# Conv input product of a diffusion layer on one Trainium2 core: tokens stationary, 512 weight columns streamed, `mod_w` loads in twos

## The chip, the cores and the metric

The kernel runs on one core of a Trainium2 chip. The time is device microseconds (us) from the first to the last instruction of the core, with the launch around it, and the figure that counts is the median of the timed runs. Engines by their names in the profile: PE (TensorE, matmuls; PEld are its weight loads), DVE (VectorE), ACT (ScalarE), POOL (GpSimd), SP (SyncE, which issues the large loads).

## What is computed

One layer over 256 latent tokens of width 2048, in float32: a modulation vector from `c`, a gated short convolution, a layer norm, and a mixture of 16 experts with top 2 of one group.

```
mod = split(silu(c) @ mod_w + mod_b, 6)                      # six vectors of 2048
h = x * (1 + mod[1]) + mod[0]
gate_b, gate_c, val = split(h @ w_in, 3)                     # w_in: 2048 x 6144
o = (gate_b * depthwise_conv3(gate_c * val, w_conv)) @ w_out # w_out: 2048 x 2048
x = layer_norm(ALPHA * x + mod[2] * o)
x = layer_norm(ALPHA * x + mod[5] * moe(x * (1 + mod[4]) + mod[3]))
```

The change is in the product `h @ w_in` (the "input product") and in what stands around it: the gating, the convolution over tokens, and the loads of `mod_w`.

## The kernel before

**Loads.** All weights come through a ring of six SBUF slots (`get`, `RING`), each 3072 float32 per partition, 1.57 MB. SP issues the loads in the order of a list `steps`; a slot is loaded again only when its last reader is done, and a load that waits for its slot holds up all later ones on SP.

**Steps.** The first part of the kernel, up to about 520 us, is that list. Each step has a load and a piece of work: `cin_step` (input product), `cout_step` (output product, `co`), `gemv_cols` and `gemv_rows` (a block of 512 columns of `mod_w` times the vector `silu(c)`, `gv`; its 16 row blocks come in three loads of 6, 6 and 4). `merge` deals the steps of one list between those of another. The input product can only run for those rows of `h` whose modulation is known, so there are five stages over the inner dimension (`KGS` = 2, 2, 4, 4, 4 blocks of 128): while stage i is multiplied for a first half of the channels, the `mod_w` blocks for stage i+1 are loaded and multiplied (`h_mods`), and partial sums are added up in SBUF (`acc_step`, tiles `acc`). The second half of the channels (`full_steps`) then runs with all of `h` at hand and sums in PSUM. The rest of the blocks of `mod_w` (`late`; `EXTRA` of them inside the stages) and the output product `co` are dealt between the steps.

**Precision.** A float32 matmul of the products is three matmuls: weights and tokens are each split into a rounded high part (ACT, `hic`, `hio`) and a low part (DVE, `loc`, `loo`), and high x high, high x low, low x high are summed. `split` does 1024 columns at a time, with two buffers for each part: the split of a piece can begin only when PE is done with the piece before the last. I call such a piece a half.

**Input product.** In `cin_step` 128 x 128 of the weights is the stationary operand and 256 tokens (`hhi`, `hlo`) are streamed, so results come out with channels on the partitions, as the convolution over tokens needs them; `conv_group` works on them directly (`u`, `v`, then `yh` and `yl` for the output product). The output product does it the other way: tokens (`yh`, `yl`) stationary, 512 weight columns streamed.

**Blocks on DVE.** Five of the late blocks of `mod_w` are not multiplied on PE but on DVE (`ON_V`): 15 multiply-adds each (`rows`). They wait in `queue`, and `split` takes two of them after each half.

**Order.** What stands behind what on one engine is not as written: a scheduler reorders the instructions of an engine when the program is built. The order stays fixed at run time, each engine goes through its own in turn.

Of the kernel before, what the change touches and what calls it, by code (L numbers as in the profile page):

```python
# [27 lines left out]
BIG = 1.0e30  # L28

RING = 6  # L30
ACC_GROUPS = 4
YB = 4
DRIP = (1, 6, 3)
EXTRA = [0, 1, 0, 0, 12]
KGS = [2, 2, 4, 4, 4]
BEFORE = 4
EARLY = 3
VN = 2
AT = 1
# [27 lines left out]
def trunk_kernel(  # L67
# [30 lines left out]
    def mm_tile(name):  # L98
        return psum.tile([P, 512], F32, tag="mm", bufs=6, name=name)
# [302 lines left out]
    def mm3(ps, whi, wlo, ahi, alo, start, stop):  # L402
        TE.matmul(ps, whi, ahi, start=start, stop=False)  # L403
        TE.matmul(ps, whi, alo, start=False, stop=False)  # L404
        TE.matmul(ps, wlo, ahi, start=False, stop=stop)  # L405

    def cin_step(k0, nk, g, pss, first, last, then=None, hook=None):
        n = nk * 256

        def load(w):  # L410
            wv = w[:, : 3 * n].rearrange("p (a t c) -> p a t c", a=3, c=256)
            for a in range(3):
                nc.sync.dma_start(wv[:, a], cin[:, a, k0 : k0 + nk, g * 256 : (g + 1) * 256])

        def work(w):
            if first:
                pss.extend(mm_tile(f"ci{k0}_{g}{a}") for a in range(3))
            for a in range(3):
                hi, lo = split(w[:, a * n : (a + 1) * n], n, f"c{k0}_{g}{a}")
                if a == 1 and hook:  # L420
# [7 lines left out]
            if then:  # L428
                then(pss)

        return load, work

    def conv_group(g, gb, gc, val):

        u = p1.tile([P, 2, T], F32, tag="e", bufs=3, name=f"u{g}")
        V.tensor_mul(u.rearrange("p b t -> p (b t)"), val, gc)
        v = p1.tile([P, 2, T], F32, tag="e", bufs=3, name=f"v{g}")
        for b in range(2):
            ct = g * 2 + b
# [7 lines left out]
        V.tensor_mul(vf, vf, gb)  # L447
        yh = p1.tile([P, 2, T], F32R, tag="yhi", bufs=YB, name=f"yh{g}")
        yl = p1.tile([P, 2, T], F32R, tag="ylo", bufs=YB, name=f"yl{g}")
        S.copy(yh.rearrange("p b t -> p (b t)"), vf)  # L450
        V.tensor_sub(yl.rearrange("p b t -> p (b t)"), vf, yh.rearrange("p b t -> p (b t)").bitcast(F32))
        yhi[g], ylo[g] = yh, yl

    accs = [big_tile(f"acc{g}").rearrange("p (a t) -> p a t", a=3) for g in range(ACC_GROUPS)]
    mod2b = p1.tile([P, D], F32, name="mod2b")
    stats = const.tile([P, 2, 4, 6], F32, name="stats")

    def acc_step(i, g, hook=None):
        def then(pss):
            for a in range(3):  # L460
                if i == 0:
                    V.tensor_copy(accs[g][:, a, :], pss[a][:, :])
                else:
                    V.tensor_add(accs[g][:, a, :], accs[g][:, a, :], pss[a][:, :])  # L464
            if i == len(KGS) - 1:
                conv_group(g, accs[g][:, 0, :], accs[g][:, 1, :], accs[g][:, 2, :])
        return cin_step(sum(KGS[:i]), KGS[i], g, [], True, True, then, hook)

    def full_steps(g):
        def then(pss):  # L470
            gcs = p1.tile([P, 512], F32, tag="e", bufs=3, name=f"gcs{g}")
            S.copy(gcs, pss[1][:, :])
            conv_group(g, pss[0][:, :], gcs, pss[2][:, :])
        pss = []
        return [cin_step(kg * 4, 4, g, pss, kg == 0, kg == 3, then if kg == 3 else None) for kg in range(4)]

# [107 lines left out]

    def h_mods(i):
        c0, n = sum(KGS[:i]) * P, KGS[i] * P
        return list(gemv_cols(0, c0, n)) + list(gemv_cols(1, c0, n))

    def h_hook(i):
        def fn():
# [17 lines left out]

    def merge(a, b):

        out, nb = [], 0
        for i, st in enumerate(a):
            out.append(st)
            while nb < (i + 1) * len(b) // len(a):
                out.append(b[nb])
                nb += 1
        return out

    steps = h_mods(0) + [(None, lambda w: h_hook(0)())]
    late = [st for m in (2, 3, 4) for q in range(4) for st in mods(m, q)]
    last = [st for q in range(4) for st in mods(5, q)]
    NK = len(KGS)
    for i in range(NK):
        nxt = h_mods(i + 1) if i < NK - 1 else []
        nxt += late[sum(EXTRA[:i]) : sum(EXTRA[: i + 1])]
        steps += merge([acc_step(i, g) for g in range(ACC_GROUPS - 1)], nxt)
        steps += [acc_step(i, ACC_GROUPS - 1, h_hook(i + 1) if i < NK - 1 else None)]
    late = late[sum(EXTRA) :]  # L630
    rest = []
    for g in range(ACC_GROUPS, CG):
        fs = last_cin = full_steps(g)
        qt = [cout_step(g - 4, j) for j in range(4)] if 4 <= g < 7 else []
        if g < 6:
            rest += fs[:2] + qt + fs[2:]
        elif g == 6:
            rest += fs
        else:
            rest += fs + qt_last  # L640
        qt_last = qt
    steps += merge(rest[:-BEFORE], late) + [(None, lambda w: router_prep())]
# [673 lines left out]
```

## Time and profile before

| | us |
|---|---|
| median of 3 runs | 1300.05 (1299.6 to 1301.11) |
| profiled execution, its own time | 1300.78 |
| its span, first to last instruction | 1299.1 |
| first part: steps up to the router | up to about 520 |
| experts | about 520 to 1270 |

A busy PE is not PE at its peak: matmuls overlap, so a PE that is busy all the time can still be waiting between matmuls. Start-to-start distances say what one matmul costs in a stream. Names are those of the program with buffer numbers left out: `ci<-hhi,hic` writes the sums of the input product from the tokens' and the weights' high parts. An idle time is given with what ended it.

### The profile page before, as it was taken

What the parts mean: (1) busy time and instruction counts of PE and PEld (TensorE: products, weight loads), DVE (VectorE), ACT (ScalarE), POOL (GpSimd) and SP (SyncE); (2) the same over time, 40 slices, a digit from 0 to 9 for tenths busy, and PEclk for the clock granted to TensorE, in tenths of its full rate; (3) what the DMA queues carried; (4) which work ended last, traced back from release to release, by engine and by line L of the source; (5) the groups of instructions that cost most, each with busy time, mean ns of one, the idle gap of its engine ahead of it and who ended that gap; (6) DMA issues with size and microseconds to landing.
All of it is one profiled execution on the core that took longest, in us unless ns stands there. A gap on an engine that the chain in (4) does not pass through costs nothing. (4 is left out here: it accounts for less than half of the span.)

```text
span 1299.1 us, 19675 instructions
## 1 busy us (share of the span) xinstructions
PE 1148.7 (88%) x7871; PEld 755.3 (58%) x7871; DVE 669.4 (52%) x1257; ACT 364.7 (28%) x634; POOL 36.2 (3%) x66
## 2 busy tenths in 40 slices
PE   4999999999999999887789997999689997789982
PEld 2778886878699965543257543674157443444352
DVE  1664555687879978442255642573146431123226
ACT  1332333433344424240035312451026110100020
POOL 1000000000300030000000000000000000000000
PEclk7999999999999999698899999999899999899996
DMA  9999889899999878899998899999999899999991
GB/s 310 372 388 396 301 286 399 305 315 338 348 316 347 306 270 282 366 412 430 429 409 349 321 422 428 405 360 376 428 430 425 338 429 429 429 428 430 429 396 69
DMA packets 151105, 475.61 MB, mean 366 GB/s; under 512 B 11000, under 2 KB 70104, under 8 KB 126688
## 3 DMA queue, kind: packets, MB, share of 16 engines
q1 hardware_dynamic: 145984, 471.89, 92.4%
q10 hardware_dynamic: 5024, 2.40, 0.6%
q8 instruction: 64, 1.05, 0.3%
q14 instruction: 33, 0.27, 0.1%
HBM read 472.16 MB, written 2.10 MB: 365 GB/s over the span
## 5 line engine op out<-in xcount | busy, mean ns | idle before, releaser
L986 PE MATMUL gue<-w,xgp 128*32 128x384 f32 (+1 forms) x1664 | 219.1, 538 | 63.6 <-DMA w<-in_ex_w_up_dram 55.7
L403 PE MATMUL ci<-hhi,hic 128*128 128x256 f32 x768 | 219.6, 287 | 2.3 <-ACT hic L395 1.4
L405 PE MATMUL ci<-hhi,loc 128*128 128x256 f32 x768 | 217.3, 284 | 3.8 <-DVE loc L396 3.6
L404 PE MATMUL ci<-hlo,hic 128*128 128x256 f32 x768 | 216.9, 283 | 0.6 <-DVE hlo L390 0.4
L986 PEld LDWEIGHTS gue<-w,xgp 128*32 128x32 f32 (+1 forms) x1664 | 81.3, 123 | 198.3 <-issue 90.1
L403 PEld LDWEIGHTS ci<-hhi,hic 128*128 128x128 f32 x768 | 145.4, 190 | 14.6 <-issue 8.4
L395 ACT CAST hic<-w 128x1024 fp32r<-128x1024 f32 (+1 forms) x108 | 102.5, 953 | 178.8 <-PE ci L404 153.3
L405 PEld LDWEIGHTS ci<-hhi,loc 128*128 128x128 f32 x768 | 145.1, 189 | 9.4 <-DVE loc L396 6.6
L404 PEld LDWEIGHTS ci<-hlo,hic 128*128 128x128 f32 x768 | 145.5, 189 | 5.4 <-DVE hlo L390 2.3
L396 DVE TENSOR_TENSOR loc<-w,hic 128x1024 fp32r<-128x1024 f32 (+1 forms) x108 | 118.5, 1106 | 34.2 <-ACT hic L395 32.0
L733 DVE TENSOR_TENSOR parts<-w,parts 128x384 fp32r<-128x384 f32 (+1 forms) x168 | 97.8, 612 | 56.8 <-ACT parts L732 55.5
L732 ACT CAST parts<-w 128x384 fp32r<-128x384 f32 (+1 forms) x168 | 89.7, 559 | 79.2 <-PE gue L983 59.5
L1005 ACT COPY gse<-gue 128x384 f32<-128x384 f32 x16 | 7.7, 481 | 313.9 <-PE gue L986 313.9
L858 PEld LDWEIGHTS gap<-ohp,xt 128*128 128x128 f32 x512 | 66.0, 209 | 22.6 <-issue 16.0
L858 PE MATMUL gap<-ohp,xt 128*128 128x128 f32 (+2 forms) x512 | 70.2, 294 | 5.0 <-DVE xgp L826 5.0
L986 PE MATMUL gue<-w,xfp 128*128 128x384 f32 x192 | 71.5, 495 | 1.7 <-DMA w<-in_ex_w_gate_dram 1.7
L273 PE MATMUL gv<-w,sT 128*32 128x512 f32 (+1 forms) x416 | 57.1, 567 | 7.5 <-DMA w<-in_mod_w_dram 7.5
L464 DVE TENSOR_TENSOR acc<-acc,ci 128x512 f32<-128x512 f32 x48 | 32.9, 686 | 58.8 <-PE ci L405 58.6
L1092 DVE TENSOR_TENSOR Y<-dne,m 32x512 f32<-32x512 f32 (+3 forms) x84 | 40.7, 484 | 37.4 <-PE dne L944 34.1
L278 DVE SCALAR_TENSOR_TENSOR rows<-w,sT,rows 128x512 f32<-128x512 f32 x75 | 57.8, 771 | 1.3
L558 PE MATMUL co<-loo,yh 128*128 128x512 f32 x128 | 51.5, 402 | 3.0 <-DVE loo L396 3.0
L826 DVE TENSOR_SCALAR xgp<-gap,GB 128x32 f32<-128x32 f32 (+1 forms) x104 | 31.5, 314 | 43.6 <-ACT xgp L824 43.1
(311 smaller groups left out, 1452.7 us busy)
## 6 DMA issues: line engine op xcount, KB each, us to landing
w<-in_ex_w_gate_dram SPq DMA_DIRECT2D x64, 1536.0 KB, 14.7
w<-in_ex_w_up_dram SPq DMA_DIRECT2D x64, 1536.0 KB, 16.8
w<-in_ex_w_down_dram SPq DMA_DIRECT2D x60, 1536.0 KB, 14.0
w<-in_mod_w_dram SPq DMA_DIRECT2D x48, 1536.0 KB, 8.9
w<-in_conv_in_w_dram SPq DMA_DIRECT2D x84, 512.0 KB, 6.9
w<-in_mod_w_dram SPq DMA_DIRECT2D x22, 1024.0 KB, 8.2
w<-in_conv_out_w_dram SPq DMA_DIRECT2D x16, 1024.0 KB, 6.6
w<-in_conv_in_w_dram SPq DMA_DIRECT2D x24, 256.0 KB, 6.3
```

The source lines that it names most:

```text
L273: TE.matmul(box["ps"][32 * g : 32 * g + 32, :n], sT[:, kt : kt + 1].to_broadcast([P, 32]), ws, start=kt < 4, stop=kt >= 12)
L278: V.scalar_tensor_tensor(out=box["r"][:, :n], in0=ws, scalar=sT[:, kt : kt + 1], in1=box["r"][:, :n], op0=ALU.mult, op1=ALU.add)
L395: S.copy(hi[:, :n], src)
L396: V.tensor_sub(lo[:, :n], src, hi[:, :n].bitcast(F32))
L403: TE.matmul(ps, whi, ahi, start=start, stop=False)
L404: TE.matmul(ps, whi, alo, start=False, stop=False)
L405: TE.matmul(ps, wlo, ahi, start=False, stop=stop)
L558: TE.matmul(pso[h][:, :], yh[:, k, a:b], wl, start=False, stop=False)
L732: S.copy(hi[:, :n], src)
L733: V.tensor_sub(lo[:, :n], src, hi[:, :n].bitcast(F32))
L858: TE.matmul(ps[:, k * n : (k + 1) * n], xn[:, h, (k0 + k) * P : (k0 + k + 1) * P], oh[:, h, :n], start=h == 0, stop=h == 1)
L986: TE.matmul(dst, big[0][:, KF.index(kt), :] if cc == 128 else xg[:, kt, :cc], src, start=st_, stop=sp_)
```

## The change

**Input product.** `cin_step` now holds 128 tokens (`hhi`, `hlo`) stationary and streams 512 weight columns, for two halves of the tokens and part by part (gate_b, gate_c, val): 1152 matmuls of 512 columns take the place of 2304 of 256. Results have tokens on the partitions. `accs` has two groups of 512 channels where there were four of 256; a group's slots are now full in every stage (two steps for a stage of 4). `full_steps` runs one part at a time over all of the inner dimension, in slots of 6, 6 and 4 blocks.

**Convolution.** `conv_group` first transposes u (already gate_c x val) and gate_b back to channels on partitions: 8 matmuls of 128 x 128 with `ident` (`uT`, `bT`) for 256 channels, 64 in all; ACT and DVE then read them from PSUM. The product gate_c x val is done before, on the `acc` tiles. A group's two pairs are two calls, both put in `pending` and run after the next step.

**Loads of `mod_w`.** `runs` binds the first two loads of a block together; `merge` deals such pairs. `EXTRA` goes from [0, 1, 0, 0, 12] loads to [0, 0, 0, 0, 8] pairs and singles (12 loads), so one load that stood in the second stage comes later.

```diff
-    def cin_step(k0, nk, g, pss, first, last, then=None, hook=None):
...
-                for b in range(2):
-                    for k in range(nk):
-                        o = k * 256 + b * P
-                        mm3(pss[a][:, b * T : (b + 1) * T], hi[:, o : o + P], lo[:, o : o + P],
-                            hhi[:, k0 + k, :], hlo[:, k0 + k, :],
-                            first and k == 0 and b == 0, last and k == nk - 1 and b == 1)
+    def cin_step(entries, g, pairs, k_first, k_last, then, hook=None):
...
+                for k in range(0, nk, 2):
+                    hi, lo = split(w[:, o + k * 512 : o + k * 512 + 1024], 1024, f"c{g}{a}{k0 + k}")
+                    for j in range(2):
+                        kt = k0 + k + j
+                        wh, wl = hi[:, j * 512 : j * 512 + 512], lo[:, j * 512 : j * 512 + 512]
+                        for h in range(2):
+                            ps, s = pairs[a][h], slice(h * P, (h + 1) * P)
+                            TE.matmul(ps[:, :], hhi[:, kt, s], wh, start=kt == k_first, stop=False)
+                            TE.matmul(ps[:, :], hhi[:, kt, s], wl, start=False, stop=False)
+                            TE.matmul(ps[:, :], hlo[:, kt, s], wh, start=False, stop=kt == k_last)
...
-    def conv_group(g, gb, gc, val):
-        u = p1.tile([P, 2, T], F32, tag="e", bufs=3, name=f"u{g}")
-        V.tensor_mul(u.rearrange("p b t -> p (b t)"), val, gc)
+    def conv_group(g, pr=0):
+        u = mm_tile(f"uT{g}{pr}")
+        gb = mm_tile(f"bT{g}{pr}")
+        for a, ps in ((2, u), (0, gb)):
+            for b in range(2):
+                for h in range(2):
+                    c = (pr * 2 + b) * P
+                    TE.transpose(ps[:, b * T + h * P : b * T + h * P + P], accs[g][h][:, a, c : c + P], ident)
...
+        if pr == 0:
+            pending.append(lambda: conv_group(g, 1))
...
-    def acc_step(i, g, hook=None):
+    def acc_steps(i, g, hook=None):
...
+            if i == len(KGS) - 1 and a == 2:
+                for h in range(2):
+                    V.tensor_mul(accs[g][h][:, 2, :], accs[g][h][:, 2, :], accs[g][h][:, 1, :])
+                pending.append(lambda: conv_group(g))
...
     def full_steps(g):
...
+            for h in range(2):
+                o = accs[g][h]
+                if a == 2:
+                    V.tensor_mul(o[:, 2, :], pair[h][:, :], o[:, 1, :])
+                else:
+                    S.copy(o[:, a, :], pair[h][:, :])
+            if a == 0:
+                pending.append(lambda: conv_group(g))
...
+        return [cin_step([(a, k0, nk)], g, pairs, 0, KT - 1, then)
+                for a in (1, 2, 0) for k0, nk in ((0, 6), (6, 6), (12, 4))]
...
+    def runs(sts):
+        return [sts[:-1], sts[-1:]]
...
+    rest = fs[:3] + co[0] + fs[3:6] + co[1] + fs[6:] + last_cin + co[2]
```

Three places of the fixed order follow, of before and of after.

On PE, in the stage of the fourth pair of `mod_w` blocks: the matmuls of the first block (`gv` of columns 1536) stand in pieces in before, with products between; these are the second and third piece (five matmuls of a load of which the first stood sixty rows ahead, and six of the next load).

```order
L405 MATMUL ci_02_1386<-hhi,loc_02_1444 128x256
L273 MATMUL gv_1536_1478<-w_1146,sT 32x512 x5
L273 MATMUL gv_1536_1478<-w_1238,sT 32x512 x6
L403 MATMUL ci_10_1495<-hhi,hic_10_1498 128x256
L404 MATMUL ci_10_1495<-hlo,hic_10_1498 128x256
L405 MATMUL ci_10_1495<-hhi,loc_10_1499 128x256
```

After:

```order
L429 MATMUL ci_1054<-loc_1056,hhi 128x512
L430 MATMUL ci_1054<-hic_1055,hlo 128x512
L271 MATMUL gv_1536_1073<-w_852,sT 32x512 x6
L271 MATMUL gv_1536_1073<-w_860,sT 32x512 x6
L428 MATMUL ci_1053<-hic_1091,hhi 128x512
L429 MATMUL ci_1053<-loc_1092,hhi 128x512
```

The twelve matmuls of two loads now stand in one run; in before they are runs of 1 and 11.

On DVE, late in the second half of the channels, where a block is multiplied on DVE (`rows`) beside the input product (`loc` is the low part of a half), before:

```order
L396 TENSOR_TENSOR loc_70_4141<-w_3914,hic_70_4140 128x1024
L278 SCALAR_TENSOR_TENSOR rows_3918<-w_3824,sT,rows_3918 128x512 x2
L396 TENSOR_TENSOR loc_71_4171<-w_3914,hic_71_4170 128x1024
L278 SCALAR_TENSOR_TENSOR rows_4230<-w_3928,sT,rows_4230 128x512 x2
L396 TENSOR_TENSOR loc_72_4201<-w_3914,hic_72_4200 128x1024
L278 SCALAR_TENSOR_TENSOR rows_4230<-w_3928,sT,rows_4230 128x512 x2
L396 TENSOR_TENSOR loc_70_4243<-w_4035,hic_70_4242 128x1024
L278 SCALAR_TENSOR_TENSOR rows_4230<-w_3928,sT,rows_4230 128x512
```

After:

```order
L394 TENSOR_TENSOR loc_2917<-w_2772,hic_2916 128x1024
L276 SCALAR_TENSOR_TENSOR rows_2935<-w_2776,sT,rows_2935 128x512
L276 SCALAR_TENSOR_TENSOR rows_2935<-w_2778,sT,rows_2935 128x512 x4
L250 TENSOR_REDUCE gs_512_2942<-gc_512_2937 128x4
L276 SCALAR_TENSOR_TENSOR rows_2935<-w_2778,sT,rows_2935 128x512
L252 SCALAR_TENSOR_TENSOR modT<-gs_512_2942,T1t 128x4
L394 TENSOR_TENSOR loc_2950<-w_2834,hic_2949 128x1024
L394 TENSOR_TENSOR loc_2968<-w_2834,hic_2967 128x1024
```

Two `rows` stand between halves in before; here five, six with the one behind `gs`, stand between the last half of one slot (`w_2772`) and the first of the next (`w_2834`).

On DVE, where the input product ends and the third quarter of the output product begins (`loo` is the low part of a half of `co`; `rtB`, `rsums`, `rtw` and `gbm` prepare the router), before:

```order
L396 TENSOR_TENSOR loo_4539<-w_4240,hio_4538 128x1024
L451 TENSOR_TENSOR yl_4438<-v_4429,yh_4437 128x512
L485 TENSOR_TENSOR B_101<-B_101,modT 128x16
L565 TENSOR_TENSOR t_4504<-co_4470,mod2b 128x512
L488 TENSOR_TENSOR rtB<-rtw,B_101 128x512
L565 TENSOR_TENSOR t_4507<-co_4471,mod2b 128x512
L489 TENSOR_REDUCE rsums<-rtB 128x20
L490 TENSOR_TENSOR rtw<-rtw,G_100 128x512
L396 TENSOR_TENSOR loo_4555<-w_4240,hio_4554 128x1024
L491 TENSOR_REDUCE rsums<-rtw 128x20
L396 TENSOR_TENSOR loo_4581<-w_4331,hio_4580 128x1024
```

After, the last rows ahead of the half `loo_3355`:

```order
L457 SCALAR_TENSOR_TENSOR v_3255<-uT_3245,T2t,v_3255 128x255
L520 TENSOR_TENSOR rtw<-rtw,G_100 128x512
L460 TENSOR_TENSOR v_3255<-v_3255,bT_3246 128x512
L521 TENSOR_REDUCE rsums<-rtw 128x20
L595 TENSOR_TENSOR t_3320<-co_3286,mod2b 128x512
L464 TENSOR_TENSOR yl_3264<-v_3255,yh_3263 128x512
L595 TENSOR_TENSOR t_3323<-co_3287,mod2b 128x512
L526 TENSOR_TENSOR rb<-rb,rsum 128x20
L527 COPY rsum<-rsum 128x20
L538 TENSOR_TENSOR gbm_3337<-gbT,gbmask 16x512
L538 TENSOR_TENSOR gbm_3343<-gbT,gbmask 16x512
L394 TENSOR_TENSOR loo_3355<-w_3114,hio_3354 128x1024
```

In before one half (`loo_4555`) has seven rows between it and the half ahead. After, `loo_3355` has 22: these eleven, and eleven more like them between the half ahead of it and the first row shown (the end of one pair's convolution, the start of the next one's, `gs`, `modT`, `G`, `B`, `rtB`, one `rsums`).

## Rows read from the trace of the kernel before

**Rows 1.** The page: busy tenths of PE and DMA in 40 slices of the span

```profile
PE   4999999999999999887789997999689997789982
...
DMA  9999889899999878899998899999999899999991
```

**Rows 2.** By stages: window, us, busy PE PEld DVE ACT POOL, PEclk, DMA, GB/s

```profile
28.70:84.60 55.90, 54.12 (x437) 41.82 (x438) 33.13 (x61) 17.37 (x31) 0.00 (x0) 0.96 1.04 373
84.60:132.00 47.40, 46.17 (x359) 36.84 (x357) 27.29 (x38) 16.40 (x20) 0.00 (x0) 1.00 1.07 398
132.00:178.80 46.80, 46.53 (x370) 38.12 (x369) 26.39 (x37) 15.91 (x18) 0.00 (x0) 1.00 0.88 318
178.80:240.50 61.70, 57.26 (x430) 40.38 (x429) 38.56 (x55) 21.98 (x31) 0.00 (x0) 1.00 0.95 348
240.50:449.00 208.50, 204.98 (x1493) 181.99 (x1493) 169.49 (x211) 82.42 (x92) 13.54 (x8) 1.00 0.90 319
449.00:520.00 71.00, 69.16 (x384) 44.49 (x386) 56.19 (x99) 26.57 (x31) 15.13 (x11) 1.00 0.81 286
```

**Rows 3.** Timeline of PE (start, us, instruction): ten products apart, then twelve

```profile
288.90 0.28 PE L403 MATMUL ci<-hhi,hic 128*128 128x256 f32 x1
...
290.08 0.28 PE L404 MATMUL ci<-hlo,hic 128*128 128x256 f32 x1
...
271.19 0.39 PE L557 MATMUL co<-hio,yh 128*128 128x512 f32 x1
...
273.91 0.39 PE L557 MATMUL co<-hio,yh 128*128 128x512 f32 x1
```

**Rows 4.** The same timeline: four transposes and the matmul behind them

```profile
274.59 0.60 PE L250 MATMUL gc<-ident,rows 128*128 128x128 f32 x4
274.95 0.47 PE L557 MATMUL co<-hio,yh 128*128 128x512 f32 x1
```

**Rows 5.** Lines of the first part, by shape: the transposes of the tokens

```profile
L382 PE MATMUL xT<-ident,xt 128*128 128x128 f32 x32 | 5.4, 297 | 0.0
```

**Rows 6.** Timeline of PE: two runs of `gv`, each with the row behind

```profile
145.22 2.77 PE L273 MATMUL gv<-w,sT 128*32 128x512 f32 x22
147.92 0.39 PE L403 MATMUL ci<-hhi,hic 128*128 128x256 f32 x1
...
159.20 1.91 PE L273 MATMUL gv<-w,sT 128*32 128x512 f32 x12
161.04 0.39 PE L405 MATMUL ci<-hhi,loc 128*128 128x256 f32 x1
```

**Rows 7.** Timeline of DVE: a half, three `rows`, the next half

```profile
439.43 1.22 DVE L396 TENSOR_TENSOR loc<-w,hic 128x1024 fp32r<-128x1024 f32 x1 [0.17 <-ACT hic L395]
440.57 2.32 DVE L278 SCALAR_TENSOR_TENSOR rows<-w,sT,rows 128x512 f32<-128x512 f32 x3
442.81 1.22 DVE L396 TENSOR_TENSOR loc<-w,hic 128x1024 fp32r<-128x1024 f32 x1
```

**Rows 8.** Timeline of DVE at the start of the third quarter of `co`

```profile
453.03 0.68 DVE L451 TENSOR_TENSOR yl<-v,yh 128x512 fp32r<-128x512 f32 x1
...
454.91 0.68 DVE L565 TENSOR_TENSOR t<-co,mod2b 128x512 f32<-128x512 f32 x1
455.52 0.74 DVE L489 TENSOR_REDUCE rsums<-rtB 128x20 f32<-128x320 f32 x1
456.16 1.76 DVE L490 TENSOR_TENSOR rtw<-rtw,G 128x512 f32<-128x512 f32 x1
457.85 1.21 DVE L396 TENSOR_TENSOR loo<-w,hio 128x1024 fp32r<-128x1024 f32 x1
```

**Rows 9.** Timeline of PE at the same place, idle times in brackets

```profile
456.86 0.73 PE L557 MATMUL co<-hio,yh 128*128 128x512 f32 x2 [0.69 <-ACT hio L395]
457.52 1.04 PE L300 MATMUL gv<-w,sT 128*32 128x512 f32 x2
459.12 0.50 PE L558 MATMUL co<-loo,yh 128*128 128x512 f32 x1 [0.55 <-DVE loo L396]
```

More of the change, by code (lines that the diff above doesn't have):

```diff
@@ L30 @@
 RING = 6
-ACC_GROUPS = 4
 YB = 4
 DRIP = (1, 6, 3)
-EXTRA = [0, 1, 0, 0, 12]
+EXTRA = [0, 0, 0, 0, 8]
 KGS = [2, 2, 4, 4, 4]
@@ new lines, in trunk_kernel @@
+    accs = [big_tile(f"acc{i}").rearrange("p (a c) -> p a c", a=3) for i in range(4)]
+    accs = [accs[0:2], accs[2:4], accs[2:4], accs[2:4]]
+    def conv_group(g, pr=0):
[6 more added lines that the diff above has]
+                    TE.transpose(ps[:, b * T + h * P : b * T + h * P + P], accs[g][h][:, a, c : c + P], ident)
+        u = u.rearrange("p (b t) -> p b t", b=2)
+        v = p1.tile([P, 2, T], F32, tag="e", bufs=3, name=f"v{g}{pr}")
@@ L454, in trunk_kernel, with then @@
-    accs = [big_tile(f"acc{g}").rearrange("p (a t) -> p a t", a=3) for g in range(ACC_GROUPS)]
+        yhi[g * 2 + pr], ylo[g * 2 + pr] = yh, yl
+        if pr == 0:
+            pending.append(lambda: conv_group(g, 1))
     mod2b = p1.tile([P, D], F32, name="mod2b")
     stats = const.tile([P, 2, 4, 6], F32, name="stats")
-    def acc_step(i, g, hook=None):
-        def then(pss):
-            for a in range(3):
+    def acc_steps(i, g, hook=None):
+        def then(a, pair):
+            for h in range(2):
+                o = accs[g][h][:, a, :]
@@ L461, in then @@
                 if i == 0:
-                    V.tensor_copy(accs[g][:, a, :], pss[a][:, :])
+                    V.tensor_copy(o, pair[h][:, :])
                 else:
[L464 to L467, printed above, removed]
-    def full_steps(g):
[L470 to L475, printed above, removed]
+                    V.tensor_add(o, o, pair[h][:, :])
@@ new lines, in then @@
+            if i == len(KGS) - 1 and a == 2:
+                for h in range(2):
+                    V.tensor_mul(accs[g][h][:, 2, :], accs[g][h][:, 2, :], accs[g][h][:, 1, :])
+                pending.append(lambda: conv_group(g))
+        k0, nk = sum(KGS[:i]), KGS[i]
+        if nk == 2:
+            es = [[(a, k0, 2) for a in range(3)]]
+        else:
+            es = [[(0, k0, 4), (1, k0, 2)], [(1, k0 + 2, 2), (2, k0, 4)]]
+        pairs = {}
+        return [cin_step(e, g, pairs, k0, k0 + nk - 1, then, hook if e is es[-1] else None) for e in es]
@@ new lines, in full_steps, with then @@
+    def full_steps(g):
+        def then(a, pair):
+            for h in range(2):
+                o = accs[g][h]
+                if a == 2:
+                    V.tensor_mul(o[:, 2, :], pair[h][:, :], o[:, 1, :])
+                else:
+                    S.copy(o[:, a, :], pair[h][:, :])
+            if a == 0:
+                pending.append(lambda: conv_group(g))
+        pairs = {}
+        return [cin_step([(a, k0, nk)], g, pairs, 0, KT - 1, then)
+                for a in (1, 2, 0) for k0, nk in ((0, 6), (6, 6), (12, 4))]
@@ L588, in h_mods @@
         c0, n = sum(KGS[:i]) * P, KGS[i] * P
-        return list(gemv_cols(0, c0, n)) + list(gemv_cols(1, c0, n))
+        return runs(list(gemv_cols(0, c0, n))) + runs(list(gemv_cols(1, c0, n)))
     def h_hook(i):
@@ L611, in merge @@
     def merge(a, b):
-        out, nb = [], 0
+        out, n, nb = [], 0, sum(len(s) for s in b)
+        b = list(b)
         for i, st in enumerate(a):
             out.append(st)
-            while nb < (i + 1) * len(b) // len(a):
-                out.append(b[nb])
-                nb += 1
-        return out
-    steps = h_mods(0) + [(None, lambda w: h_hook(0)())]
-    late = [st for m in (2, 3, 4) for q in range(4) for st in mods(m, q)]
+            while b and n < (i + 1) * nb // len(a):
+                n += len(b[0])
+                out += b.pop(0)
+        return out
+    def runs(sts):
+        return [sts[:-1], sts[-1:]]
+    steps = [st for r in h_mods(0) for st in r] + [(None, lambda w: h_hook(0)())]
+    late = [r for m in (2, 3, 4) for q in range(4) for r in runs(mods(m, q))]
     last = [st for q in range(4) for st in mods(5, q)]
```

62 lines of the change are left out of this document (25 added, 37 removed).

## Prediction

> **What bounds the kernel now.** I read the page's slices first: from slice 17 on DMA stands at 9 tenths in all but three slices and the last, while PE falls to 6 to 8 again and again; ahead of that PE has nines nearly throughout [rows 1]. The experts wait for their weights, the first part for PE. So the question is whether the change moves the moment at which the experts' loads get going, and that is set by the first part. There I cut the timeline at the stages [rows 2]. In the first two the DMA share is 1.04 and 1.07: nothing more comes in, and PE (54.12 of 55.90 us busy) is busy because its work just fits the loads. From 132 us on the share is 0.88, 0.95, 0.90 and 0.81, and PE is busy 46.53 of 46.80, 57.26 of 61.70, 204.98 of 208.50 and 69.16 of 71.00 us: PE sets the pace, and a load waits for its slot until PE has read what is in it. The granted clock is 1.00 from 84.6 us on, the 2.4 GHz level, and both kernels keep PE as full, so I let the clock alone. Since DMA is full behind the first part, what that part gains or loses I carry to the end at full size. PE's rows are pipelined, so all costs below are distances between starts, not the rows' own lengths.
>
> **The change part by part.**
>
> *A, streaming.* Ten 256-column products take 290.08 − 288.90 = 1.18 us, 0.118 each; twelve 512-column products of the output product, in the form that the input product now gets, take 273.91 − 271.19 = 2.72, 0.227 each [rows 3]. Removed: 2304 x 0.118 = 271.9 us; added: 1152 x 0.227 = 261.5. That is −10.4 us, on PE and so on the path, except in the first two stages, where DMA has the last word (E). Half as many weight loads follow from it, but they lie beside the matmuls (PEld 181.99 beside PE 204.98 [rows 2]) and I count nothing for them.
>
> The Trainium skill ("TensorE: Matmul & The Clock Gate", section "Back-to-back issue gap") gives a gap of N/2.4 + 2.5 ns for a single matmul at full clock, 109 ns for 256 columns and 216 for 512. By that 1152 doubled matmuls would save only about 2.4 us, 8 less than by the rows (an estimate from the page); the trace's two distances, 118 and 227 ns, both lie about 10 ns above the rule, so the fixed share of a matmul is larger here, and I go by the rows.
>
> *B, transposes.* 64 of 128 x 128 are added. Four of them start 0.36 us ahead of the next product [rows 4], 0.09 each: 5.8 us. With a little for changing between kinds I take +6.4. Below 5.8 there is no reason to go; the upper end is the transposes of the tokens, whose rows are 0.297 long [rows 5], 19 us if nothing overlapped. Rows 4 shows the same shape in the same stream, so I stay near it. ACT and DVE read the results in place of the product's own PSUM, with the same shapes.
>
> *C, the `mod_w` products.* They run on PE as groups of four, side by side in columns of the array, and a run of fewer than four costs a whole group: 11 matmuls take 147.92 − 145.22 = 2.70 us and 6 take 161.04 − 159.20 = 1.84, that is 3 and 2 groups, 0.86 for a group [rows 6] (x22 and x12 count two records for each). Before, the order has 43 runs with 92 groups; after, with two loads bound together, 35 runs with 84. Eight groups fewer are −7 us. Its bounds are 0, if the records hide a wait, and −7.
>
> *D, bursts on DVE.* `split` still needs DVE once for each half, and PE has two buffers to work from. In before the order spreads `rows` by twos or threes: three of them take 442.81 − 440.57 = 2.24 us, 0.75 each, and PE goes on [rows 7]. After, the order has five places where five to seven `rows`, with `gs` or `t` among them, stand ahead of the first half of a slot (of which `loc_2950` is shown above), and a sixth, `loo_3355`, with 22 rows. Prices: `rows` 0.75, `t` 0.61, `rtw` 1.69 [rows 7, 8], the small rows some 0.1. The five come to 6.0, 5.7, 6.4, 5.2 and 5.6 us, the sixth to 10.8. How much is covered, the one such burst of before tells: 457.85 − 453.03 = 4.82 us between halves [rows 8], for which PE shows idle times of 0.69 and 0.55, and 1.0 of `gv` between [rows 9]; the first `co` rows behind a wait run at longer distances too, which I put at 0.5. So a stall of 1.75 at 4.82, with 1.0 of other work: 4.82 − 1.75 − 1.0 = 2.1 us of cover. With it, and the 0.4 to 1.2 us of transposes and the like that PE has at each place, the stalls are 3.5 + 3.2 + 3.1 + 2.7 + 2.7 + 7.2 = 22.3 us. Before pays at its own places, which fall away: at some six of them with the 1.24 us shown in rows 9, 7. Net **+15**. Bounds: 0, if DVE gets ahead (the first rival), and 22, if before pays elsewhere and keeps paying. I take the middle-high value since the price comes from the nearest place there is, one burst of the same kind with the same engine waiting.
>
> *E, start.* One 1.57 MB load leaves the second stage, where loads are the limit: 1.57 MB at 373 GB/s [rows 2] is 4.2 us. But since slots are bound and dealt in twos, the last step of a stage has 36 products of 0.227 us behind its last load, 8.2 us, where it had 36 of 0.118, 4.2. The two nearly meet: **−2**, from 0 to −4.
>
> *F, slots that wait for DVE.* A block for DVE is loaded into the same ring; its slot comes free only when the last of its `rows` is done, and SP waits there with all later loads behind it. Where `rows` come late, the load behind them (of the input product, 7 to 8 us before it is needed) comes late. Rows of before show no such wait of PE for a load in the middle of the part. Between 0 and 4, I take **+2**.
>
> *Nothing* is counted for the additional `u` products on DVE (the same work in other places) and for ACT's copies: ACT is busy 82.42 of 208.50 us [rows 2].
>
> Sum: −10.4 + 6.4 − 7 + 15 − 2 + 2 = +4. On the profiled execution, 1300.78 us, that is 1304.8; the median of the three runs stands 0.73 below it, so 1304.0.
>
> **Rivals.**
>
> *R1, the bursts are absorbed (faster).* What decides is whether DVE enters a burst with both buffers of PE filled and whether the first half's load was there early. DVE is busy 169.49 of 208.50 us [rows 2], so it has 39 us in which to get ahead; the buffers stop it from getting further than two halves, about 5.4 us of PE work (24 products of 0.227), which is as long as the bursts other than the sixth. If all that counts, D is 0: −10.4 + 6.4 − 7 − 2 + 2 = −11, 1289. For it speaks rows 7, where three `rows` cost no wait; against it rows 8 and 9, where 4.82 us did.
>
> *R2, bursts in full and slots late.* Before's own stalls stay and F is at its end: −10.4 + 6.4 − 7 + 22.3 − 2 + 4 = +13, 1313. For it speaks that a burst ends in the first half of a new slot, so the slots behind it come free late too; against it that DMA has room there (share 0.90 [rows 2]).
>
> *R3, the streaming is worth far more.* If 512 columns cost no more than 0.131 us, 1152 products would take 151 us, 121 less; loads would then be the limit, and bringing the shares of 0.88, 0.95, 0.90 and 0.81 up to the 1.05 of the start [rows 2] gives 8 + 6 + 30 + 16 = 60 us: some 1241. Rows 3 shows 0.227 in this very form, twelve times in a row, so this has next to no weight. The Trainium skill (same page and section) states 131 ns for 512 columns in a sustained stream of weight loads and matmuls; by that rule this rival would be the forecast, and the trace disagrees with it.
>
> **How the numbers follow.** A measurement of this kernel tells some 0.2 % from no change, 2.6 us: "same" is 1297.5 to 1302.7. Chances: forecast 0.55 (1299 to 1309), R1 0.23 (1284 to 1294), R2 0.20 (1309 to 1318), R3 0.02. Of the forecast 0.33 lies above 1302.7, 0.18 within and 0.04 below; R1 is faster but for 0.02; R2 is slower. Faster 0.04 + 0.21 + 0.02 = 0.27, same 0.18 + 0.02 = 0.20, slower 0.33 + 0.20 = 0.53. The range leaves out half of R1 (0.115), R3 (0.02) and a third of R2 (0.07): 1289 to 1315.
>
> **What would show it.** A: 512-column `ci` products 0.227 apart. B: 64 transposes, each eight of them about 0.7 us ahead of the next product. C: runs of 12 `gv` at 2.6 us, 8 groups less. D: idle times of PE put down to DVE `loc` or `loo` of 2.5 to 3.5 us at five places and 7 at the half `loo_3355`, in the half of the part from 240 us on; if they stay under 1 us, R1 holds. E: the second stage ends by 2 us earlier. F: idle times of PE put down to a DMA of `w` in the middle of the part. Wrong would be the whole frame if the experts' loads did not follow the first part one to one.

## The result, and the profile after

| | before | after |
|---|---|---|
| median | 1300.58 us (4 runs, 1299.6 to 1302.83) | 1314.12 us (4 runs, 1313.3 to 1318.56) |
| ratio to before, 95 % interval | | 1.0109 (1.0082 to 1.0136) |
| profiled execution, its span | 1300.78, 1299.1 | 1313.3, 1311.5 |
| first product of the stages 1 to 5 (us) | 28.9, 54.4, 85.9, 135.3, 182.2 | 26.4, 51.5, 81.8, 126.6, 171.0 |
| first product of the second half of the channels | 243.3 | 238.3 |
| last product of the input product | 446.7 | 460.5 |
| last `co` product, the end of the first part | 504.55 | 524.16 |
| first expert product (`gue`) | 546.40 | 557.37 |

The changed kernel is slower, by 13.5 us, 1.1 %. One execution of e1 below took 3868 us, where its nine others took 1295 to 1308, and is left out of e1's numbers.

The starts come from the timeline of PE, of one execution of each kernel. They say where it happens: up to the fifth stage the change gains 11.2 us (182.2 to 171.0), of which 2.4 lie ahead of the first product; the fifth stage gives 6.2 back (61.1 us become 67.3), the second half of the channels costs 18.8 (203.4 to 222.2), the rest of `co` 5.8 (57.9 to 63.7). That is +19.6 at the end of the first part. In front of the experts 8.6 us come back (41.8 to 33.2).

The page of after, the lines that answer to [rows 1]:

```profile
PE   4999998999899989986779997899589998789983
...
DMA  9999989699799768999998899999999899999992
```

DMA now has 6 and 7 in slices in which it had 8 and 9: the loads wait longer for their slots (SP waits 387 us from the third stage to the last `co` product, in before 315). The stretches of [rows 2], after (window, us, then busy time of PE, PEld, DVE, ACT, POOL, granted clock, DMA share, GB/s):

```profile
28.70:84.60 55.90, 52.36 (x302) 34.21 (x303) 36.37 (x59) 17.25 (x22) 0.00 (x0) 1.00 1.06 404
...
178.80:240.50 61.70, 55.39 (x274) 30.31 (x273) 29.62 (x41) 18.51 (x25) 0.00 (x0) 0.97 0.96 360
240.50:449.00 208.50, 194.12 (x872) 144.05 (x871) 162.59 (x201) 76.18 (x87) 13.54 (x8) 0.98 0.82 293
449.00:520.00 71.00, 66.57 (x316) 50.60 (x314) 49.48 (x69) 23.96 (x27) 13.35 (x8) 0.95 0.76 265
```

In the line of 240.50 PE is idle 14.38 of 208.50 us, where it was idle 3.52, and the granted clock, 1.00 in before, is 0.97, 0.98 and 0.95 in the last three lines. Both are new. The idle time is at the places of the forecast. On DVE, around the half `loc_2950` (start, us, instruction, idle time ahead of it in brackets):

```profile
411.32 3.89 DVE L276 SCALAR_TENSOR_TENSOR rows<-w,sT,rows 128x512 f32<-128x512 f32 x5
415.14 0.69 DVE L250 TENSOR_REDUCE gs<-gc 128x4 f32<-128x512 f32 x1
415.75 0.74 DVE L276 SCALAR_TENSOR_TENSOR rows<-w,sT,rows 128x512 f32<-128x512 f32 x1
416.41 0.15 DVE L252 SCALAR_TENSOR_TENSOR modT<-gs,T1t 128x4 f32<-128x4 f32 x1
416.49 2.35 DVE L394 TENSOR_TENSOR loc<-w,hic 128x1024 fp32r<-128x1024 f32 x2
```

DVE does not wait here; it has 5.17 us of other work ahead of the half. PE, in the timeline of the same time, waits for it, and then does something more:

```profile
417.75 0.50 PE L429 MATMUL ci<-loc,hhi 128*128 128x512 f32 x1 [2.18 <-DVE loc L394]
...
419.41 0.63 PE L430 MATMUL ci<-hic,hlo 128*128 128x512 f32 x1
...
421.97 0.63 PE L430 MATMUL ci<-hic,hlo 128*128 128x512 f32 x1
```

From 419.41 to 421.97 six products start 0.427 us apart, where 0.23 is usual: behind the wait of 2.18 us the clock has gone to its lower level, 1.2 GHz, and it comes back at 422.4. The granted clock of the stretch, behind the busy times as above, is 0.50:

```profile
420.00:422.00 2.00, 2.00 (x7) 1.52 (x6) 0.00 (x0) 0.64 (x1) 0.00 (x0) 0.50 1.04 360
```

From 240 us to the last `co` product PE's waits are 18.8 us in sum (before: 4.7), and the clock falls five times in the first part, behind the waits at 208, 281, 418, 444 and 471 us. In before it fell at none of these places (only at the start, 0.96 in the first line of [rows 2], where loads are the limit).

The longest is the half `loo_3355`, on PE:

```profile
470.85 0.41 PE L525 MATMUL rsum<-rsums,onesF 128*128 128x40 f32 x2 [2.03 <-DVE rsums L521]
...
473.88 3.57 PE L543 MATMUL gbP<-gbmask,gbm 16*128 16x4 f32 x16 [2.40 <-DVE gbm L538]
477.38 0.80 PE L588 MATMUL co<-loo,yh 128*128 128x512 f32 x1
477.97 0.63 PE L589 MATMUL co<-hio,yl 128*128 128x512 f32 x1
```

### The profile page after: what moved, and what is told of

The parts are those of the page before. It is cut to its first block, busy times and chain, and to the rows that moved or that the text cites. A ratio compares the mean times of both kernels' runs of the same rounds, so it can differ in the third digit from the quotient of the medians.

```text
span 1311.5 us, 17344 instructions
## 1 busy us (share of the span) xinstructions
PE 1150.2 (88%) x6783; PEld 703.1 (54%) x6783; DVE 670.8 (51%) x1245; ACT 363.8 (28%) x626; POOL 36.6 (3%) x66
## 5 line engine op out<-in xcount | busy, mean ns | idle before, releaser
L429 PE MATMUL ci<-loc,hhi 128*128 128x512 f32 x384 | 155.6, 406 | 10.6 <-DVE loc L394 10.6
L428 PE MATMUL ci<-hic,hhi 128*128 128x512 f32 x384 | 151.5, 406 | 5.2 <-ACT hic L393 4.4
L430 PE MATMUL ci<-hic,hlo 128*128 128x512 f32 x384 | 153.4, 401 | 0.0
L394 DVE TENSOR_TENSOR loc<-w,hic 128x1024 fp32r<-128x1024 f32 x96 | 117.6, 1230 | 59.2 <-ACT hic L393 58.4
L393 ACT CAST hic<-w 128x1024 fp32r<-128x1024 f32 x96 | 100.0, 1047 | 154.2 <-PE ci L430 116.6
L429 PEld LDWEIGHTS ci<-loc,hhi 128*128 128x128 f32 x384 | 73.1, 191 | 35.1 <-DVE loc L394 17.6
L428 PEld LDWEIGHTS ci<-hic,hhi 128*128 128x128 f32 x384 | 72.4, 191 | 32.0 <-ACT hic L393 7.6
L430 PEld LDWEIGHTS ci<-hic,hlo 128*128 128x128 f32 x384 | 73.1, 190 | 16.6
L271 PE MATMUL gv<-w,sT 128*32 128x512 f32 (+1 forms) x416 | 51.3, 566 | 7.2 <-DMA w<-in_mod_w_dram 7.2
L393 ACT CAST hio<-w 128x1024 fp32r<-128x1024 f32 x32 | 33.6, 1048 | 72.4 <-PE co L589 66.9
```

The lines of the kernel that those rows point to most:

```text
L271: TE.matmul(box["ps"][32 * g : 32 * g + 32, :n], sT[:, kt : kt + 1].to_broadcast([P, 32]), ws, start=kt < 4, stop=kt >= 12)
L428: TE.matmul(ps[:, :], hhi[:, kt, s], wh, start=kt == k_first, stop=False)
L429: TE.matmul(ps[:, :], hhi[:, kt, s], wl, start=False, stop=False)
L430: TE.matmul(ps[:, :], hlo[:, kt, s], wh, start=False, stop=kt == k_last)
```

## The experiments

Each ran beside the kernel before on the same chip. The fourth column is the sum of PE's waits in the timeline from 240 us to the last `co` product, of the profiled execution; the ratio is to the kernel before, with its interval.

| | median, us | ratio | waits, us | last `co`, us |
|---|---|---|---|---|
| before | 1300.58 | | 4.7 | 504.55 |
| after | 1314.12 | 1.0109 (1.0082 to 1.0136) | 18.8 | 524.16 |
| e1_single | 1302.38 | 1.0000 (0.9973 to 1.0027) | 6.3 | 507.03 |
| e2_before_twos | 1305.75 | 1.0030 (1.0010 to 1.0049) | 11.3 | 507.79 |
| e3_fill | 1316.33 | 1.0112 (1.0079 to 1.0145) | 16.2 | 522.80 |
| e4_vn1 | 1316.60 | 1.0123 (1.0093 to 1.0154) | 16.1 | 523.39 |
| e5_after_no_dve | 1313.59 | 1.0095 (1.0061 to 1.0128) | 3.7 | 521.37 |
| e6_before_no_dve | 1313.90 | 1.0101 (1.0069 to 1.0132) | 0.2 | 521.61 |
| e7_s15_hp | 1296.33 | 0.9964 (0.9949 to 0.9979) | 4.6 | 505.18 |
| e8_after_hp | 1306.83 | 1.0055 (1.0030 to 1.0079) | 14.7 | 512.71 |
| e9_before_hp | 1297.86 | 0.9974 (0.9957 to 0.9992) | 6.0 | 504.51 |

Executions of one kernel differ by up to 13 us (before: 1296.3 to 1305.4 in 19 runs, e8: 1300.6 to 1314.1 in 10), so the medians are compared by their intervals, and where the time goes is read from the last `co` product of the profiled execution. That is one execution of each kernel; how far this product moves between executions of one kernel no run shows.

### Loads one by one (e1)

```diff
-EXTRA = [0, 0, 0, 0, 8]
+EXTRA = [0, 1, 0, 0, 12]
...
-        return [sts[:-1], sts[-1:]]
+        return [[st] for st in sts]
```

> The changed kernel with the loads of mod_w dealt one by one again, EXTRA as before (0, 1, 0, 0, 12). Theory (the loss is waits of PE for DVE, since two bound loads put their rows in one burst ahead of the next slot's first half, and the clock falls behind each long wait): the order now has one half with more than 2 us of rows too many (loo_3371, 2.8) where it had six; the waits fall by some 16 us, and with the clock staying at 1.00 another 5 to 8 go, against 1 to 2 for the column groups that come back. Of these 20 to 22 us the stretch in front of the experts may give back up to 6, as it did between before and after: 1292 to 1299 us. Rival (the products with 512 columns and the transposes themselves cost the time): 1310 to 1318 us, as the changed kernel.

The first part ends 17.1 us earlier than in the changed kernel, and the waits are back from 18.8 to 6.3. The longest wait behind 240 us is one that before has too, and the clock stays at 1.00 to the end of the first part. The wait in before, then that of e1 and its last `co` product:

```profile
345.72 0.50 PE L558 MATMUL co<-loo,yh 128*128 128x512 f32 x1 [1.58 <-DVE loo L396]
...
344.70 0.50 PE L588 MATMUL co<-loo,yh 128*128 128x512 f32 x1 [1.73 <-DVE loo L394]
...
507.03 0.39 PE L589 MATMUL co<-hio,yl 128*128 128x512 f32 x1
```

The rival is out: this kernel has the new product and the transposes. The median, 1302.4, lies above the 1292 to 1299 that I expected (its runs go from 1295.3 to 1308.2); the profiled execution, the fastest of them, took 1295.25. By the median, what the first part gained did not all arrive at the end.

### Loads in twos alone (e2)

```diff
-EXTRA = [0, 1, 0, 0, 12]
+EXTRA = [0, 0, 0, 0, 8]
...
-        return list(gemv_cols(0, c0, n)) + list(gemv_cols(1, c0, n))
+        return runs(list(gemv_cols(0, c0, n))) + runs(list(gemv_cols(1, c0, n)))
...
+    def runs(sts):
+
+        return [sts[:-1], sts[-1:]]
...
-    steps = h_mods(0) + [(None, lambda w: h_hook(0)())]
-    late = [st for m in (2, 3, 4) for q in range(4) for st in mods(m, q)]
+    steps = [st for r in h_mods(0) for st in r] + [(None, lambda w: h_hook(0)())]
+    late = [r for m in (2, 3, 4) for q in range(4) for r in runs(mods(m, q))]
...
```

> The kernel before, with the one part alone that deals the loads of mod_w in twos (EXTRA 0, 0, 0, 0, 8). Theory (bursts): the order now has a half with 4.2 us and one with 3.6 us of rows too many, which before had not; worked through, waits grow by 6 us while the column groups give 1, and each of the two waits may bring the clock down once, 1.7 us each: first part 5 to 8 us longer, of which up to 6 may come back in front of the experts: 1301 to 1309 us. Rival (binding loads in twos does only good, by fewer column groups): 1295 to 1299 us.

1305.75 us: the theory's side. The last `co` product comes 3.2 us later, less than the 5 to 8 that I expected, though the waits grew by 6.5. A burst on DVE ahead of a half of `co`:

```profile
269.23 3.11 DVE L278 SCALAR_TENSOR_TENSOR rows<-w,sT,rows 128x512 f32<-128x512 f32 x4
272.26 1.29 DVE L565 TENSOR_TENSOR t<-co,mod2b 128x512 f32<-128x512 f32 x2
...
275.48 2.35 DVE L396 TENSOR_TENSOR loo<-w,hio 128x1024 fp32r<-128x1024 f32 x2
```

and PE waits for it:

```profile
276.75 0.50 PE L558 MATMUL co<-loo,yh 128*128 128x512 f32 x1 [3.03 <-DVE loo L396]
```

With e1 this makes a square of four, at the last `co` product: neither part 504.55, the product alone 507.03, the twos alone 507.79, both 524.16. Alone they cost 2.5 and 3.2 us; together 19.6. The rest, 13.9 us, belongs to neither: it is what the fixed order makes of the two together. The ratios of the whole time say the same, more coarsely: 0.0 and 0.3 % alone, 1.1 % together.

### No block of `mod_w` on DVE (e5 and e6)

```diff
-ON_V = [[0, 1, 0, 1], [0, 1, 1, 1]]
+ON_V = [[0, 0, 0, 0], [0, 0, 0, 0]]
```

> The changed kernel with no block of mod_w on DVE (ON_V all 0): PE multiplies the five blocks too, 20 us more work there, and no rows stand between the halves. Theory (the changed kernel loses to before by the bursts of rows): the five places lose their waits, only the half behind the router's preparation keeps one, some 9 us; waits 14 us less and the clock falls once instead of five times: first part 0 to 5 us longer than in the changed kernel, 524 to 529 us at the last co product, and no more than 5 us behind the kernel before in the same form (e6): 1312 to 1320 us. Rival (the difference to before does not hang on DVE): first part 20 us longer than in e6, 1324 to 1334 us.

> The kernel before with no block of mod_w on DVE (ON_V all 0), the partner of e5. PE has 20 us more work and some 7 us less of waits: 1309 to 1316 us, with the last co product at 514 to 519 us. Theory (bursts): at most 5 us faster than e5. Rival: 13 to 20 us faster than e5.

Without the `rows` the two kernels are equal: 1313.59 and 1313.90 us, 521.4 and 521.6 at the last `co` product. (I had expected 524 to 529 and 514 to 519: the sizes missed, on both sides.) The 13.5 us between them hang on the rows that DVE works off, but not on the waits alone. From the third stage to the last `co` product, PE's waits and what the low clock adds to its rows make a difference of 23.7 us between after and before and of 7.4 between e5 and e6. The `gv` rows make one of −2.5 there and −7.2 here: with five more blocks on PE, binding the loads saves more. The one long wait that stays in e5 behind 240 us is that of the router's preparation:

```profile
468.33 0.41 PE L525 MATMUL rsum<-rsums,onesF 128*128 128x40 f32 x2 [2.90 <-DVE rsums L521]
```

### Position alone (e8)

```diff
-        S.copy(hi[:, :n], src)
-        V.tensor_sub(lo[:, :n], src, hi[:, :n].bitcast(F32))
+        with tc.high_priority(150):
+            S.copy(hi[:, :n], src)
+            V.tensor_sub(lo[:, :n], src, hi[:, :n].bitcast(F32))
```

> The changed kernel, loads in twos as they are, with nothing but the order of the engines changed: the two instructions of split go ahead of what else is ready when the order is made. Theory (position alone): the bursts ahead of loo_2031 (3.4 us too many) and loo_3355 (7.3, now 1.0) go, the other four stay, worked through 7 us less waits and two falls of the clock fewer, 3 to 5 us: last co product at 512 to 516 us, 1302 to 1308 us. Rival (waits only move, as in e4): 521 to 525, 1311 to 1318 us.

The work and the loads are those of the changed kernel; only the order of the engines differs. The last `co` product comes at 512.7, 11.5 us earlier, the median is 1306.8, with an interval of the ratio below that of the changed kernel, and the clock falls three times in place of five. At the place of `loo_3355` the rows now have halves between them, on DVE (two rows are left out between the three):

```profile
465.45 1.23 DVE L395 TENSOR_TENSOR loo<-w,hio 128x1024 fp32r<-128x1024 f32 x1
...
467.18 0.70 DVE L521 TENSOR_TENSOR rtw<-rtw,G 128x512 f32<-128x512 f32 x1
...
468.38 1.23 DVE L395 TENSOR_TENSOR loo<-w,hio 128x1024 fp32r<-128x1024 f32 x1
```

and PE shows no wait there; the one of 2.30 us at 281 is gone too. The other four places keep theirs, as expected, but not as they were: two of them grew, to 3.41 us at 328.18 and to 3.45, and a new wait of 1.65 came at 303.40. On PE:

```profile
415.64 0.50 PE L430 MATMUL ci<-loc,hhi 128*128 128x512 f32 x1 [3.45 <-DVE loc L395]
```

So the waits fell by 4.1 us only; less low clock is another 4.5 (4.3 us in place of 8.8). Position alone is worth 11.5 of the 19.6 us; with e1 and e5 it is shown as the cause of the larger part.

### One row behind each half (e4): a miss

```diff
-VN = 2
+VN = 1
```

> The changed kernel with one of the DVE multiply-adds taken behind each half in place of two (VN = 1), loads still in twos. Theory (bursts): worked through, the order keeps two halves with some 3 us too many (loo_2031, loc_2935) and one of 1.9, and has lost those of 2359, 2781, 3119 and the 7 us of 3355: waits 10 us less and three falls of the clock fewer, 5 to 7 us, of which up to 6 may come back in front of the experts: 1297 to 1304 us. Rival (the work on DVE is the same in sum, so the same time is lost elsewhere): 1311 to 1317 us.

The theory's forecast fell: 1316.6 us, and 16.1 us of waits are left. The two bursts that were to stay did: PE waits 2.30 us at 283.27, and 0.91 and 0.55 at 416.20 and 417.47, behind seven `rows`. Of the other four, two gave way to waits of another kind. DVE, ahead of a late half:

```profile
327.52 1.37 DVE L595 TENSOR_TENSOR t<-co,mod2b 128x512 f32<-128x512 f32 x2 [3.68 <-PE co L589]
328.81 0.17 DVE L250 TENSOR_REDUCE gs<-gc 128x4 f32<-128x16 f32 x1
...
330.12 1.76 DVE L394 TENSOR_TENSOR loo<-w,hio 128x1024 fp32r<-128x1024 f32 x1
```

PE at the same place:

```profile
331.94 0.51 PE L588 MATMUL co<-loo,yh 128*128 128x512 f32 x1 [2.43 <-DVE loo L394]
```

DVE itself stood still for 3.68 us, since `t`, which needs the finished sums of `co`, is ahead of `loo` in its order; the half that PE wants next is behind an instruction that waits for PE. The same comes again at 440.15, where DVE waits 3.73 us for `gc` of PE, and PE then 1.23 for `hic` and 1.03 for `loc` behind it. A burst is too much work ahead of a half; this is a wait ahead of it. My working counted only work, so it saw the places of the first kind go and none of the second come. That is not all: the clock fell twice in place of five times, 4.0 us in place of 8.8, and yet the first part ends only 0.8 us earlier, since the rows of `co`, `gv` and the router's preparation take 5.8 us longer. Why is open.

### Fillers in the wait (e3)

```diff
             ps = aux_tile("rsum")
+            for _ in range(2):
+                TE.matmul(ps[:, 64:512], ident, t3.rearrange("p k c -> p (k c)")[:, :448], start=True, stop=True)
...
             TE.transpose(pt[:KT, P : 2 * P], B3, ident)
+            for _ in range(3):
+                TE.matmul(ps[:, 64:512], ident, rtw.rearrange("p k c -> p (k c)")[:, :448], start=True, stop=True)
```

> The changed kernel with five additional matmuls of 448 columns, whose results nobody reads, where PE waits 2.03 and 2.40 us ahead of the half loo_3355 (two on rtB, three on rtw). Theory (the wait is one cost, the fall of the clock to 1.2 GHz behind it another): the wait stays, but the granted clock stays at 1.00 there; the 16 small gbP matmuls take 1.7 us in place of 3.57 and the twelve products behind them 2.7 us in place of 4.0: the first part is 2.5 to 3.5 us shorter, the whole 1310 to 1313 us. Rival (the low clock only shows where PE would wait anyway and costs nothing): no change, 1313 to 1316 us, or longer by the fillers, up to 4 us.

The total tells nothing (1316.3 where 1310 to 1313 was expected; its interval holds the changed kernel's), and the second filler itself had to wait 1.55 us, and the clock did fall. But it was back by 475.6 us, ahead of `gbP`, and the timeline of PE shows what that is worth:

```profile
471.46 4.18 PE L535 MATMUL rsum<-rtw,ident 128*128 128x448 f32 x6 [1.55 <-DVE rsum L529]
475.57 1.94 PE L547 MATMUL gbP<-gbmask,gbm 16*128 16x4 f32 x16
477.45 0.50 PE L592 MATMUL co<-loo,yh 128*128 128x512 f32 x1
477.79 0.40 PE L593 MATMUL co<-hio,yl 128*128 128x512 f32 x1
478.02 0.39 PE L592 MATMUL co<-loo,yh 128*128 128x512 f32 x1
```

The 16 `gbP` matmuls take 1.9 us to the next start where they took 3.5, and the products start 0.23 to 0.34 apart where they started 0.43 to 0.59 apart. The low clock has a price of its own behind a wait. Whether the total would have it, this run leaves open.

### Better than both (e7), and its control (e9)

e7 is e1 with EXTRA [0, 1, 0, 0, 15] and the edit of e8; e9 is the kernel before with these two edits, its input product untouched.

> The changed kernel with the loads of mod_w one by one, 16 of the late ones inside the stages (EXTRA 0, 1, 0, 0, 15), and the two instructions of split put ahead of what else is ready when the order of the engines is made. Theory (what PE loses is set by where rows, gs and t stand ahead of a half): worked through, no half has more than 1.7 us too many; waits 6 us less than in e1: last co product at 499 to 503 us, 1289 to 1297 us, faster than before. Rival (the order only moves the waits to other places, as e4 did): last co product at 506 to 512, 1297 to 1306 us.

> The kernel before with the two edits of e7 (EXTRA 0, 1, 0, 0, 15, and the two instructions of split ahead of what else is ready), its input product as it was. Theory (the order alone makes e7 faster than before; the new product in itself gives next to nothing, since its 512-column products take 0.232 us and the transposes 7 us): e9 gains as much on before as e7 did on e1, some 2 to 7 us in the first part: last co product at 498 to 503 us, 1292 to 1298 us, equal to e7 within 3 us. Rival (the new product is what makes e7 faster): e9 stays at 1299 to 1303 us, e7 faster than it by 4 us or more.

e7 is faster than before, 0.9964 (0.9949 to 0.9979). But e9 is too, 0.9974 (0.9957 to 0.9992), and the two can't be told apart: as expected, it is not the new product that makes it. Which of the two edits does is not shown, and where, I did not expect: their first parts end at 505.2 and 504.5, no earlier than that of before and behind the 498 to 503 expected, since new waits for `loc` came ahead of the second half of the channels (2.20 us at 240.30 in e7, 2.44 at 243.13 in e9). The gain lies behind the first part, in the stretch that differs from execution to execution, and I have not separated it from that.

## Why the prediction was right, and where its steps were off

The sign, the mechanism of D and the range held; the likeliest time was 10 us short. That the range held is luck in part: carried to the end one to one, as the prediction does it, the 19.6 us of the first part would have come to 1320 us, outside 1289 to 1315. What brought the time back is the stretch in front of the experts, which the prediction has nothing on.

Term by term, at the end of the first part. E is taken from the first product of the first stage to that of the third, the terms below the start from there to the last `co` product; rows are counted by their distance to the next start, without the waits, and at the full clock (what the low clock adds has its own line).

| step | forecast | measured |
|---|---|---|
| ahead of the first product | 0 | −2.4 |
| E start | −2 | −1.6 |
| A streaming | −10.4 | −4.6 |
| B transposes | +6.4 | +7.3 |
| C `mod_w` on PE | −7 | −2.5 |
| D waits for DVE, from 240 us on | +15 | +14.1 |
| F slots | +2 | 0 |
| clock | 0 | +8.8 |
| waits ahead of 240 us | 0 | +0.8 |
| all other rows of PE | 0 | −0.3 |
| sum | +4 | +19.6 |

Ahead of the first product both kernels do the same work, so those 2.4 us are not the change's; the clock was low there up to 33.4 us in before and up to 23.1 in after.

**A was mis-sized.** The form is that of the output product, but `ci` products start 0.233 us apart, not 0.227: sixteen take 197.56 − 193.83 = 3.73 us.

```profile
193.83 0.40 PE L429 MATMUL ci<-loc,hhi 128*128 128x512 f32 x1
...
197.56 0.39 PE L430 MATMUL ci<-hic,hlo 128*128 128x512 f32 x1
```

In the median `ci` products start 0.118 us apart before and 0.232 after; in the mean, with the longer distances at the change of a half or of the kind of row, 0.1225 and 0.2405 from the third stage on: 247.0 us become 242.4. The `co` products of the same kernel stay at 0.227 in the median. What the 5 ns are is open. So rows of the same form in another product were not the price of these: at 0.118 and 0.227 the stages from the third on should have gained 9.1.

Of the two forms of rule that I weighed from the Trainium skill ("TensorE: Matmul & The Clock Gate", section "Back-to-back issue gap"), neither holds. By the gap of a single matmul, N/2.4 + 2.5 ns, all products gain 2.9 us (I wrote 2.4), an estimate from the page; the trace's 0.118 and 0.232 lie 9 and 16 ns above it, and 4.6 us came from the third stage on alone. The rival R3, from the page's 131 ns for 512 columns, is out by the 0.232.

**B held.** Eight transposes start 0.96 us ahead of what follows, where I wrote 0.7, and within a run 0.109 apart in the median; the 64 take 7.3 us to the next starts:

```profile
203.54 0.60 PE L448 MATMUL uT<-ident,acc 128*128 128x128 f32 x4
203.97 0.60 PE L448 MATMUL bT<-ident,acc 128*128 128x128 f32 x4
204.50 1.91 PE L298 MATMUL gv<-w,sT 128*32 128x512 f32 x12
```

**C held in kind, and was too large.** The groups became fewer: busy time of the blocks of 512 columns in the first part fell from 44.4 us to 38.9. By the distances to the next start, all `gv` rows take 2.5 us less from the third stage on (53.95 to 51.50), where PE sets the pace, not 7; 1.8 more are saved in the first two stages, where the loads do. The group of lines before, then after, by shape (count, busy us, mean ns, idle):

```profile
L273 PE MATMUL gv<-w,sT 128*32 128x512 f32 x288 | 44.4, 599 | 0.0
...
L271 PE MATMUL gv<-w,sT 128*32 128x512 f32 x288 | 38.9, 598 | 0.0
```

**D held, to the place, and by luck in its net.** All bracketed waits behind 240 us grew by 18.8 − 4.7 = 14.1. The six halves named carry 15.1 of them (2.30, 1.74, 1.99, 2.18, 1.56 + 0.87, 2.03 + 2.40), where I had 22.3 (the six prices add up to 22.4, and the sixth takes 1.5 us of other work of PE off, more than the 1.2 stated); against that, before's own waits hardly fell away (3.7 us stand at other places, 4.7 in before), where I had taken off 7, more than before has there in all. So the price from one burst of before (2.1 us of cover, [rows 8, 9]) found the places and was too high, the rebate was too, and the two errors nearly cancel. What D left out is a seventh burst ahead of 240 us: on DVE the convolution of the first group stands ahead of the half there, and PE waits 1.47 and 1.53 us for `hic` and `loc` where it waited 0.76 and 0.76.

**The clock is the step that failed.** I wrote that both kernels keep PE as full, and let it alone. But it fell five times in the first part, each time behind waits of 1.5 to 2.4 us, and at none of the places where PE had no wait. Seven or eight products at 0.427 in place of 0.233 are 1.5 us each time, and the fifth, with `gbP` 1.6 us slower and six slow products, 2.8: about 9 us, 8.8 by the table. To each us that the waits grew by the low clock added some 0.6 in this execution. It is no fixed price: behind the waits of 1.74 at 330.64 and 1.99 at 392.45 it did not fall, and two waits of 1.5 us near 210, the same in five kernels, brought it down in three of them (after, e4, e8) and not in e3 and e5.

**R2** came to 1313, next to what was measured, with half of its way: before's own waits did stay for the larger part, but the bursts were not in full and no load came late. **F** did not appear: SP did wait longer for slots, but no idle time of PE behind 30 us is put down to a load in either kernel.

**One to one did not hold**, by the prediction's last line the sign that its frame is wrong. 19.6 us at the last `co` product are 11.0 at the first expert product and 12.4 in the span. Between the two PE runs the router and the first gathers (`gap`), and there the clock is low in both kernels, in before for longer. Before, then after:

```profile
520.00:530.00 10.00, 7.35 (x41) 4.42 (x37) 7.05 (x34) 3.61 (x7) 0.61 (x1) 0.75 1.00 419
530.00:540.00 10.00, 10.00 (x49) 8.60 (x41) 1.58 (x4) 0.59 (x1) 0.00 (x0) 0.50 1.00 428
540.00:550.00 10.00, 9.32 (x27) 3.63 (x31) 5.04 (x21) 3.77 (x10) 0.00 (x0) 0.56 0.77 328
```

```profile
540.00:550.00 10.00, 8.21 (x64) 5.80 (x57) 7.10 (x32) 3.82 (x8) 0.61 (x1) 0.94 1.01 428
550.00:560.00 10.00, 10.00 (x53) 6.82 (x56) 3.69 (x14) 2.38 (x6) 0.00 (x0) 0.55 1.01 429
560.00:570.00 10.00, 9.05 (x84) 2.92 (x76) 4.13 (x20) 2.21 (x5) 0.00 (x0) 1.00 1.00 426
```

By the granted clock 2.5, 5.0 and 4.4 of each ten us are lost in before, 11.9; after 0.6 and 4.5, 5.1. That is up to 6.8 of the 8.6 us that come back, an estimate, since PE is not busy all the time there. The same stretch took 35.2 us in e1 and 39.7 in e2, 35.0 in e5 and 32.2 in e6: it does not go by the change. It may be why totals of like kernels spread; no run shows it, since each kernel has the trace of one execution. Why the clock comes back after 10 us in one execution and after 24 in another is open.

## What to carry to other kernels

Where a fixed order feeds a busy engine from a helper with two buffers, look at the helper's row for what stands ahead of each piece that the busy engine wants next: both the sum of the work, against the cover of two buffers, and any instruction there that itself waits for the busy engine. Two edits that cost some 3 us each alone cost 20 together here, because the order that is built from both has a burst ahead of six halves, that of either alone of one or two: price the built order, not the edits. And a wait of TensorE is to be priced with the low clock that may come behind it, here some 0.6 us for each us that the waits grew by. Last, two errors that cancel in a sum are not a term that held.

## What the runs showed of the hardware

- Behind a wait of 2.18 us the 512-column products went from 0.233 to 0.427 us apart, for seven or eight of them (the granted clock at 0.50 of full, 1.2 GHz); behind waits of 3.03 us in e2 and 3.45 us in e8 they did not. The length of the wait alone does not tell.
- 256 and 512 columns cost 0.118 and 0.232 us in the median of these streams (0.1225 and 0.2405 in the mean): holding tokens and doubling the columns saves 2 %, not the 4 % that the output product's 0.227 had promised.
